# Pinning every engine to a planner's order, with four local moves, in a two-layer encoder

## The chip, the core and the metric

One core of one Trainium2 chip runs the whole program. The metric is the device time of one execution in microseconds (us); the time of a kernel is the median over its runs. The engines are named as in the profile: PE (TensorE, matrix products and transposes), ACT (ScalarE), DVE (VectorE), POOL (GpSimd) and SP (SyncE, which here only issues transfers).

## The reference

Two layers on 512 tokens of width 1024, batch 1, in float32. Each layer has four steps, each closed by a layer norm:

```
for i in range(2):
    y = swiglu(x, ffn_w_gate[i,0], ffn_w_up[i,0], ffn_w_down[i,0])    # hidden width 2816
    x = layer_norm(ALPHA*x + 0.5*y, ...)
    y = mixer_ab(x, ...) if i == 0 else mixer_c(x, ...)
    x = layer_norm(ALPHA*x + y, ...)
    y = memory_attn(x, mem, mem_w_q[i], mem_w_kv[i], mem_w_o[i])      # 4 heads into 256 memory tokens
    x = layer_norm(ALPHA*x + y, ...)
    y = swiglu(x, ffn_w_gate[i,1], ffn_w_up[i,1], ffn_w_down[i,1])
    x = layer_norm(ALPHA*x + 0.5*y, ...)
```

mixer_ab has 8 dense heads (RMS-normed, rotated q and k, 2 key heads) and 8 heads in a window of 128 tokens with a sink logit; mixer_c is a 2-D neighbourhood attention with 16 heads and a relative bias.

## The kernel before

Every float32 operand of a product is split into a rounded high part and a low part (ACT casts the high part, DVE subtracts it for the low part), and a product is three matmuls: high·high, high·low, low·high (`mm3`). x lies in four token tiles `x0` to `x3` of 128x1024; its transposes, which feed the projections, lie split in `xh` and `xl`, written by `to_features` (8 PE transposes a tile, two casts, two subtractions).

The stages run one after another: `ffn` four times, `mixer_ab` and `mixer_c` once, `memory` twice. A stage ends in `down`, which adds the last output projection to each x tile and closes it with `layer_norm` and `to_features`, tile by tile.

Weights come by SP through two large `raw` buffers (1 MB), are split into `slab` buffers, and are then used from there. There are 27 slabs of 128x1024, handed out first in, first out, in the order in which the program asks; a request waits until a slab is free. PSUM has 3 banks of kind `a`, 3 of `t` and 2 of `d`. The names in the profile are those of these buffers: `t` is also the name of the small SBUF tiles (`t2`).

Nothing is issued when the Python code runs. `Graph.record` writes down each operation with its dependencies and a cost in ns (`cost`); `emit` then plays the program as a list schedule: each engine takes, among what is ready, the operation that was written first, and `LATENCY` is added between engines. The operations are handed to the framework in the order that results. The framework's own scheduler then places them again, so that an engine's final order is not everywhere that of the planner. All recorded operations have the line of the recorder (L140), so that rows are told apart by their tiles.

At the start, `ffn_by_tokens` loads x0, then the first gate and up weights in halves, then x1 to x3, and works token tile by token tile. In `mixer_ab`, tile by tile, the keys and queries go through `rms` (square on ACT, sum on DVE, `rsqrt`, product on DVE) and `rope` (three products on DVE, a sum on POOL); `keys` and `queries` then transpose them. `padded` gives two zeroed tiles, by POOL memsets. `rsqrt` is two POOL steps, mean and eps (`tensor_scalar`) and `pow` against the constant `nhalf`. In the loop over 16 heads, `aside[n]` lists what is done behind head n: `last_columns` (the second half of the queries, four tiles, in `d` banks; its last step copies values out of the bank on ACT), shares of the output projection, and so on. In `mixer_c` the key and query parts are moved across partitions by SP's transfers (`slab<-t`), on the same queue as the weights. `memory` begins with the load of the memory, 16 transposes and 4 split pairs, behind the mixer's `down` in the order of the program.

Of the kernel before, what the change touches and what calls it, by code (L numbers as in the profile page):

```python
# [12 lines left out]
F32 = mybir.dt.float32  # L13
# [4 lines left out]
ALU = mybir.AluOpType  # L18
# [45 lines left out]
class Graph:  # L64
# [1 line left out]

    LATENCY = 90.0
    PATIENT = ("vector", "scalar")  # L70
    ENGINES = ("tensor", "vector", "scalar", "gpsimd", "sync")

    def __init__(self, nc):
        self.nc = nc
        self.ops, self.spaces, self.tiles = [], {}, {}
        for e in self.ENGINES:
            setattr(self, e, Recorder(self, e))
        self.banks, self.after = None, None
# [30 lines left out]
    @staticmethod  # L109
    def cost(engine, method, out, ins, kw):  # L110
        n = 1
        for d in (out if method != "tensor_reduce" else ins[0]).ap[1:]:
            n *= d[1]
        wide = any(z.space == bass.MemoryType.PSUM for z in ins + [out]) if engine != "sync" else False
        if method == "dma_start":
            return max(n * out.ap[0][1] * 4 / 205.0, 600.0) if engine == "sync" else 700.0
        if engine == "tensor":
            return max(n / 2.4 + 14, 111)
        small = sum(1 for z in ins if z.ap[-1][1] == 1 and n > 1)
        if engine == "vector":  # L120
            if method in ("tensor_copy", "tensor_scalar") and not wide:
                n = n / 2
            return n / 0.96 + 72 + 60 * ("accum_out" in kw)
        if engine == "scalar":
            return n / 1.2 + (90 if wide else 130) + 45 * small + 130 * ("accum_out" in kw)
        return n * {"tensor_scalar": 2.85, "memset": 1.0}.get(method, 2.17) + 110

    def record(self, engine, method, args, kw):
        kw = dict(kw)
# [35 lines left out]
    def emit(self):  # L165
        for info in self.tiles.values():
            info["left"] = len(info["users"])
            for op in info["users"]:
                op.frees.append(info)
        now = {e: 0.0 for e in self.ENGINES}  # L170
        heaps = {e: [] for e in self.ENGINES}
        ready = {e: [] for e in self.ENGINES}
        for op in self.ops:
            op.wait = len(op.deps) + len(op.frees)
            op.ready = 0.0
            for d in op.deps:
                d.users.append(op)

        def release(op, t):
            op.ready = max(op.ready, t)  # L180
            op.wait -= 1
            if op.wait == 0:
                heapq.heappush(heaps[op.engine], (op.ready, op.rank, op.index, op))

        def grant(space):

            while space.next < len(space.queue) and space.free:
                info = space.queue[space.next]
                space.next += 1
                if info["users"]:  # L190
                    t = heapq.heappop(space.free)
                    for op in info["users"]:
                        release(op, t)

        def arrive(e):
            while heaps[e] and heaps[e][0][0] <= now[e]:
                _, rank, i, op = heapq.heappop(heaps[e])
                heapq.heappush(ready[e], (rank, i, op))

        for op in self.ops:  # L200
            if op.wait == 0:
                heapq.heappush(heaps[op.engine], (0.0, op.rank, op.index, op))
        for space in self.spaces.values():
            grant(space)
        done = 0
        self.stats = []
        while done < len(self.ops):
            best = None
            for e in self.ENGINES:
                arrive(e)  # L210
                if ready[e] and e in self.PATIENT:
                    rank, _, op = ready[e][0]
                    for at, r, _, _ in heapq.nsmallest(4, heaps[e]):
                        if at < now[e] + op.ns * 0.6 and r < rank - 40:
                            now[e] = at
                            arrive(e)
                            break
                if ready[e]:
                    t = now[e]
                elif heaps[e]:  # L220
                    t = heaps[e][0][0]
                else:
                    continue
                if best is None or t < best[0]:
                    best = (t, e)
            assert best, "no instruction can start"
            t, e = best
            if not ready[e]:
                now[e] = t
                continue  # L230
            _, _, op = heapq.heappop(ready[e])
            op.call()
            self.stats.append((e, t, op))
            now[e] = t + op.ns
            end = now[e] + {"sync": 2000.0, "tensor": 160.0}.get(e, 4000.0 if op.dma else 70.0)
            done += 1
            for u in op.users:
                release(u, now[e] if e == u.engine == "tensor" else end + self.LATENCY)
            touched = set()
            for info in op.frees:  # L240
                info["left"] -= 1
                info["at"] = max(info.get("at", 0.0), end)
                if info["left"] == 0:
                    heapq.heappush(info["space"].free, info["at"] + self.LATENCY)
                    touched.add(info["space"])
            for space in touched:
                grant(space)


class Kernel:  # L250
    def __init__(self, ctx, tc, a, out):
        self.tc, self.a, self.out = tc, a, out
        self.nc = Graph(tc.nc)
        pool = lambda name, bufs, **kw: ctx.enter_context(tc.tile_pool(name=name, bufs=bufs, **kw))
        self.cst = pool("cst", 1)
        self.big = pool("big", 1)
        self.t2p = pool("t2p", 1)
        self.slp = pool("slp", 1)
        self.raw = pool("raw", 2)
        self.sm = pool("sm", 8)  # L260
        self.psp = self.nc.banks = pool("psp", 8, space=bass.MemoryType.PSUM)
        self.dram = pool("dram", 1, space=bass.MemoryType.DRAM)
        self.n = 0
# [105 lines left out]
    def rsqrt(self, sums, n, tag, mean, eps):  # L369

        nc = self.nc
        y = self.small(n, tag + "y")
        nc.gpsimd.tensor_scalar(y, sums, mean, eps, ALU.mult, ALU.add)
        nc.gpsimd.tensor_tensor(out=y, in0=y, in1=self.nhalf[:, :n], op=ALU.pow)
        return y

# [23 lines left out]
    def layer_norm(self, t, st, gb):  # L400

        nc = self.nc
        g, b = gb
        x = self.x[t]
        nmu = self.small(1, "nmu")
        nc.vector.tensor_scalar(nmu, st[:, 0:1], st[:, 1:2], -1.0 / D, ALU.add, ALU.mult)
        var = self.small(1, "var")
        nc.scalar.activation(self.junk, x, AF.Square, bias=nmu, scale=1.0, accum_out=var)
        r = self.rsqrt(var, 1, "ln", 1.0 / D, LN_EPS / ALPHA**2)
        nc.vector.scalar_tensor_tensor(out=x, in0=x, scalar=nmu, in1=g, op0=ALU.add, op1=ALU.mult)  # L410
        nc.vector.scalar_tensor_tensor(out=x, in0=x, scalar=r, in1=b, op0=ALU.mult, op1=ALU.add)

    def down_bank(self, acts, wts, t, h, coef, tag="d"):

# [47 lines left out]
    def ffn_by_tokens(self, wg, wu, first, dst):  # L462

        if first:
            self.load_x(0)
            self.to_features(0)
            self.nc.after = self.nc.ops[-1], {"scalar", "vector"}
        gate, up = self.w_cols_k(wg, 0), self.w_cols_k(wu, 0)
# [207 lines left out]
    def mixer_ab(self, ln_i, last):  # L676
# [189 lines left out]
        vb, kB, wa, acts, q = self.padded(), [], {}, [], [None]  # L866
        aside.setdefault(5, []).append(lambda: (values_turned(), kB.extend(keys(kb, True))))
        aside[6] = [values_b]
        for n in range(8):
            h, t = divmod(n, 4)  # L870
            if t == 0:
# [42 lines left out]
    def mixer_c(self, ln_i, last):  # L914
# [153 lines left out]
        for pair in range(8):  # L1068
# [16 lines left out]
            if pair < 6:  # L1085
                for t in range(2):
                    values(pair // 2 + 1, 2 * (pair % 2) + t)
            elif pair == 6:
                share(2)
        gb = self.load_ln(ln_i)  # L1090
        self.down(acts[4:], self.w_rows(w_out, 512) + self.w_rows(w_out, 768), 1.0 / ALPHA, {"gb": gb, "last": last})


    def memory(self, i, ln_i, last):
        nc, a = self.nc, self.a
        w_q, w_kv, w_o = a["mem_w_q"][i], a["mem_w_kv"][i], a["mem_w_o"][i]
        mt = []
        raw = self.tile(self.raw, [P, 2, D], F32, "raw")
        nc.sync.dma_start(out=raw, in_=a["mem"].rearrange("(m p) d -> p m d", p=P))
        for kk in range(4):  # L1100
            ps = self.transposed(
                [(j * 256 + m * P, P, raw[:, m, (2 * kk + j) * P : (2 * kk + j + 1) * P]) for j in range(2) for m in range(2)]
            )
            mt.append(self.split_t2(ps))
        memT = lambda k, lo, hi: [z[:, (k % 2) * 256 + lo : (k % 2) * 256 + hi] for z in mt[k // 2]]
        def project(head):

# [182 lines left out]
```

## Time and profile before

| | us |
|---|---|
| median of 3 runs | 2258.34 |
| lowest, highest run | 2257.48, 2258.69 |
| profiled execution, first to last instruction (its span) | 2256.3 |
| around the span, against the median of the runs | 2.0 |
| PE busy | 2206.4 |
| DVE busy | 1395.8 |
| ACT busy | 863.3 |
| POOL busy | 286.1 |
| mean granted PE clock | 0.996 |

A row of the time order reads: start, duration (merged over a run of like instructions), engine, line, operation, out<-in, shapes, xcount, and in brackets the idle time ahead of it with what ended it. The duration of merged matmuls includes the pipeline's tail, so that it is a little over count times pitch.

### The profile page before, as it was taken

What the parts mean: (1) busy time and instruction counts of PE and PEld (TensorE: products, weight loads), DVE (VectorE), ACT (ScalarE), POOL (GpSimd) and SP (SyncE); (2) the same over time, 40 slices, a digit from 0 to 9 for tenths busy, and PEclk for the clock granted to TensorE, in tenths of its full rate; (3) what the DMA queues carried; (4) which work ended last, traced back from release to release, by engine and by line L of the source; (5) the groups of instructions that cost most, each with busy time, mean ns of one, the idle gap of its engine ahead of it and who ended that gap; (6) DMA issues with size and microseconds to landing.
All of it is one profiled execution on the core that took longest, in us unless ns stands there. A gap on an engine that the chain in (4) does not pass through costs nothing.

```text
span 2256.3 us, 28354 instructions
## 1 busy us (share of the span) xinstructions
PE 2206.4 (98%) x11312; PEld 1873.9 (83%) x11312; DVE 1395.8 (62%) x2084; ACT 863.3 (38%) x1386; POOL 286.1 (13%) x391
## 2 busy tenths in 40 slices
PE   8999999899999999999999999999999999999998
PEld 7888888778798888888888888898888988888886
DVE  5666646678745756666565667366666457666653
ACT  4323333367443433333333233245544334333331
POOL 0000203434000100002100002023411001000011
PEclk9999999999999999999999999999999999999999
DMA  6333241002433331225212334235453433322241
GB/s 206 129 119 112 68 153 57 19 19 58 132 126 116 112 109 60 76 94 186 87 42 96 117 112 149 75 107 146 120 163 96 131 112 113 112 77 72 86 140 38
DMA packets 176436, 233.69 MB, mean 104 GB/s; under 512 B 7728, under 2 KB 138416, under 8 KB 176304
## 3 DMA queue, kind: packets, MB, share of 16 engines
q1 hardware_dynamic: 173232, 221.39, 31.1%
q0 software_dynamic: 3072, 10.49, 1.4%
q8 instruction: 89, 1.46, 0.3%
q14 instruction: 43, 0.35, 0.0%
HBM read 217.17 MB, written 4.19 MB: 98 GB/s over the span
## 4 chain that ended last, share of the span: by engine, by line
PE 92%; DVE 3%; ACT 2%; DMA 1%; POOL 1%; issue 1%; SPq 0%; POOLq 0%; DVEq 0%; ACTq 0%
PE a L140 55%; PE d L140 25%; PE t L140 12%; DVE slab L140 1%; DVE x L140 1%; POOL lny L140 1%; DMA slab<-t 1%; ACT junk L140 0%; DMA x<-x 0%; ACT t L140 0%; DVE t L140 0%; ACT slab L140 0%; SPq L140 0%; DMA raw<-mem_w_kv 0%; ACT xh L140 0%
## 5 line engine op out<-in xcount | busy, mean ns | idle before, releaser
L140 PE MATMUL a<-xh,slab 128*128 128x512 f32 (+1 forms) x2960 | 890.6, 382 | 0.0
L140 PEld LDWEIGHTS a<-xh,slab 128*128 128x128 f32 x2960 | 549.1, 188 | 107.0
L140 PE MATMUL d<-slab,slab 128*128 128x512 f32 (+2 forms) x2432 | 571.7, 384 | 4.3 <-DVE slab L140 1.9
L140 PE MATMUL a<-xl,slab 128*128 128x512 f32 (+1 forms) x1480 | 565.1, 382 | 0.0
L140 PEld LDWEIGHTS d<-slab,slab 128*128 128x128 f32 x2432 | 442.2, 189 | 92.9 <-DVE slab L140 4.2
L140 ACT CAST slab<-raw 128x1024 fp32r<-128x1024 f32 x316 | 320.9, 1050 | 313.4 <-DMA raw<-ffn_w_gate 144.8
L140 DVE TENSOR_TENSOR slab<-raw,slab 128x1024 fp32r<-128x1024 f32 x316 | 391.0, 1252 | 73.7 <-ACT slab L140 56.1
L140 PEld LDWEIGHTS a<-xl,slab 128*128 128x128 f32 x1480 | 278.3, 188 | 53.2
L140 DVE TENSOR_TENSOR slab<-slab,slab 128x1024 fp32r<-128x1024 f32 (+2 forms) x208 | 241.2, 1183 | 19.6 <-ACT slab L140 17.8
L140 ACT CAST slab<-slab 128x1024 fp32r<-128x1024 f32 (+1 forms) x144 | 140.1, 1000 | 237.8 <-DVE slab L140 237.5
L140 PE MATMUL a<-slab,slab 128*128 128x256 f32 (+3 forms) x1336 | 204.5, 302 | 11.7 <-DMA slab<-t 3.8
L140 ACT CAST slab<-t 128x512 fp32r<-128x512 f32 (+2 forms) x233 | 127.5, 570 | 209.6 <-DVE t L140 144.7
L140 DVE TENSOR_TENSOR slab<-a,t 128x512 f32<-128x512 f32 x56 | 38.7, 692 | 268.2 <-PE a L140 268.2
L140 PEld LDWEIGHTS a<-slab,slab 128*128 128x128 f32 x1336 | 178.8, 192 | 27.0 <-DVE slab L140 6.5
L140 DVE SCALAR_TENSOR_TENSOR x<-d,x 128x512 f32<-128x512 f32 x216 | 147.4, 685 | 48.0 <-PE d L140 47.1
L140 DVE TENSOR_TENSOR slab<-t,slab 128x512 fp32r<-128x512 f32 (+2 forms) x233 | 145.3, 648 | 24.6 <-ACT slab L140 23.8
L140 PE MATMUL t<-slab,slab 128*128 128x512 f32 (+1 forms) x648 | 151.8, 379 | 0.0
L140 POOL TENSOR_TENSOR x<-x,slab 128x512 f32<-128x512 f32 x24 | 46.0, 1947 | 834.6 <-DVE x L140 834.6
L140 ACT ACTIVATE t<-a 128x512 f32<-128x512 f32 (+3 forms) x105 | 58.1, 553 | 219.9 <-PE a L140 218.9
L140 PEld LDWEIGHTS t<-slab,slab 128*128 128x128 f32 x648 | 115.7, 188 | 24.8 <-DVE slab L140 2.1
L140 POOL TENSOR_TENSOR t<-t,l 128x256 f32<-128x256 f32 (+2 forms) x104 | 85.1, 834 | 335.8 <-DVE l L140 321.1
L140 PE MATMUL a<-slab,xh 128*128 128x256 f32 (+1 forms) x432 | 98.6, 321 | 4.0 <-ACT xh L140 3.9
(104 smaller groups left out, 1803.8 us busy)
## 6 DMA issues: line engine op xcount, KB each, us to landing
raw<-ffn_w_gate SPq DMA_DIRECT2D x40, 1024.0 KB
raw<-ffn_w_up SPq DMA_DIRECT2D x40, 1024.0 KB
slab<-ffn_w_down SPq DMA_DIRECT2D x64, 512.0 KB
raw<-ffn_w_down SPq DMA_DIRECT2D x12, 1024.0 KB
slab<-t SPq DMA_DIRECT2D x96, 128.0 KB
raw<-mem_w_kv SPq DMA_DIRECT2D x8, 1024.0 KB
raw<-mem_w_kv SPq DMA_DIRECT2D x16, 512.0 KB
raw<-mem_w_q SPq DMA_DIRECT2D x8, 1024.0 KB
```

The source lines that it names most:

```text
L140: op.call = lambda: fn(*args, **kw)
```

## The change

Six edits, all in how the work is ordered or placed; every product is the same.

1. The planner's costs and latencies are other numbers (two of the lines are shown).
2. `emit` hands each operation over with `keep_in_program_order`, so that each engine's final order is the planner's.
3. The first step of `rsqrt` is a DVE instruction, 40 in all.
4. `layer_norm` writes (x + nmu)·g into a new slab `y` instead of into x, ahead of `rsqrt`.
5. Twenty transposes of the identity into one bank stand on PE ahead of x0's.
6. `memory_turned` (load, transposes and splits of the memory) is a function of its own, called behind head 14 of `mixer_ab` and behind pair 6 of `mixer_c`.

```diff
-    LATENCY = 90.0
+    LATENCY = {"tensor": 55.0, "vector": 36.0, "scalar": 36.0, "gpsimd": 85.0, "sync": 60.0}
...
-            return max(n * out.ap[0][1] * 4 / 205.0, 600.0) if engine == "sync" else 700.0
+            return max(n * out.ap[0][1] * 4 / 300.0, 600.0) if engine == "sync" else 600.0
...
-            op.call()
+            self.tc.keep_in_program_order(op.call())
...
-        nc.gpsimd.tensor_scalar(y, sums, mean, eps, ALU.mult, ALU.add)
+        nc.vector.tensor_scalar(y, sums, mean, eps, ALU.mult, ALU.add)
         nc.gpsimd.tensor_tensor(out=y, in0=y, in1=self.nhalf[:, :n], op=ALU.pow)
...
         nc.scalar.activation(self.junk, x, AF.Square, bias=nmu, scale=1.0, accum_out=var)
+        y = self.slab(F32)
+        nc.vector.scalar_tensor_tensor(out=y, in0=x, scalar=nmu, in1=g, op0=ALU.add, op1=ALU.mult)
         r = self.rsqrt(var, 1, "ln", 1.0 / D, LN_EPS / ALPHA**2)
-        nc.vector.scalar_tensor_tensor(out=x, in0=x, scalar=nmu, in1=g, op0=ALU.add, op1=ALU.mult)
-        nc.vector.scalar_tensor_tensor(out=x, in0=x, scalar=r, in1=b, op0=ALU.mult, op1=ALU.add)
+        nc.vector.scalar_tensor_tensor(out=x, in0=y, scalar=r, in1=b, op0=ALU.mult, op1=ALU.add)
...
             self.load_x(0)
+            warm = self.ps("t")
+            for n in range(20):
+                self.nc.tensor.transpose(warm[:, :P], self.ident, self.ident)
             self.to_features(0)
...
         aside[6] = [values_b]
+        aside[14] = [self.memory_turned]
...
             elif pair == 6:
                 share(2)
+                self.memory_turned()
...
+    def memory_turned(self):
         raw = self.tile(self.raw, [P, 2, D], F32, "raw")
-        nc.sync.dma_start(out=raw, in_=a["mem"].rearrange("(m p) d -> p m d", p=P))
+        self.nc.sync.dma_start(out=raw, in_=self.a["mem"].rearrange("(m p) d -> p m d", p=P))
+        self.mt = []
         for kk in range(4):
             ps = self.transposed(
                 [(j * 256 + m * P, P, raw[:, m, (2 * kk + j) * P : (2 * kk + j + 1) * P]) for j in range(2) for m in range(2)]
             )
-            mt.append(self.split_t2(ps))
+            self.mt.append(self.split_t2(ps))
```

What stands in a row on an engine, at the places that the prediction speaks of. First ACT at the start of the program, before; raw_95 and raw_100 are the first gate and up weights, xh_83 the high part of x, t_93 and t_94 x0's transposes:

```order
2 L140 CAST slab_96<-raw_95 128x1024
3 L140 CAST slab_98<-raw_95 128x1024
4 L140 CAST slab_101<-raw_100 128x1024
5 L140 CAST xh_83<-t_93 128x4x128
6 L140 CAST xh_83<-t_94 128x4x128
7 L140 CAST slab_103<-raw_100 128x1024
```

and after:

```order
2 L140 CAST xh_83<-t_94 128x4x128
3 L140 CAST xh_83<-t_95 128x4x128
4 L140 CAST slab_97<-raw_96 128x1024
5 L140 CAST slab_99<-raw_96 128x1024
6 L140 CAST slab_102<-raw_101 128x1024
7 L140 CAST slab_104<-raw_101 128x1024
```

x0's two casts have moved ahead of all four weight casts.

POOL in mixer_ab, at the keys' last two token tiles, before; rms2y is the root of the two key heads, slab_544 the dense keys, slab_540 a tile of the window queries, slab_617 and slab_618 the zeroed value tiles:

```order
47 L140 TENSOR_TENSOR rms2y_581<-rms2y_581,nhalf_89 128x2
48 L140 TENSOR_TENSOR slab_544<-t_502_583,t_501_582 128x256
49 L140 TENSOR_TENSOR slab_540<-t_504_585,t_503_584 128x4x64
50 L140 MEMSET slab_617 128x1024
51 L140 MEMSET slab_618 128x1024
52 L140 TENSOR_SCALAR rms2y_589<-rh_588 128x2
53 L140 TENSOR_TENSOR rms2y_589<-rms2y_589,nhalf_89 128x2
54 L140 TENSOR_TENSOR slab_544<-t_510_591,t_509_590 128x256
```

and after (slab_549, slab_545, slab_622 and slab_623 are the same tiles):

```order
37 L140 TENSOR_TENSOR rms2y_586<-rms2y_586,nhalf_89 128x2
38 L140 TENSOR_TENSOR slab_549<-t_507_588,t_506_587 128x256
39 L140 TENSOR_TENSOR slab_545<-t_509_590,t_508_589 128x4x64
40 L140 TENSOR_TENSOR rms2y_594<-rms2y_594,nhalf_89 128x2
41 L140 MEMSET slab_622 128x1024
42 L140 TENSOR_TENSOR slab_549<-t_515_596,t_514_595 128x256
43 L140 MEMSET slab_623 128x1024
44 L140 TENSOR_TENSOR slab_545<-t_517_598,t_516_597 128x4x64
```

The tensor_scalar has left POOL, pow stands ahead of both memsets, and the memsets stand one on each side of the keys' sum.

PE at the end of mixer_c, where the last down projection (d), the transposes of x2 and x3 and the memory's first products meet, before; raw_2727 is the memory, t_2728 to t_2734 its transposes, a_2746 and a_2748 the first key and value projections of the memory:

```order
7834 L140 MATMUL d_2721<-slab_2693,slab_2682 128x512
7835 L140 MATMUL t_2717<-ident_78,x_6_87 128x128 x4
7836 L140 MATMUL t_2718<-ident_78,x_6_87 128x128 x4
7837 L140 MATMUL t_2728<-ident_78,raw_2727 128x128 x4
7838 L140 MATMUL a_2746<-slab_2729,slab_2737 128x256
7839 L140 MATMUL a_2748<-slab_2742,slab_2729 128x256
```

and after, where a_2771 is the first of these projections:

```order
7848 L140 MATMUL d_2754<-slab_2724,slab_2712 128x512
7849 L140 MATMUL t_2750<-ident_78,x_6_87 128x128 x4
7850 L140 MATMUL t_2751<-ident_78,x_6_87 128x128 x4
7851 L140 MATMUL d_2754<-slab_2723,slab_2712 128x512
7852 L140 MATMUL a_2771<-slab_2683,slab_2762 128x256 x2
7853 L140 MATMUL a_2771<-slab_2683,slab_2763 128x256
```

The memory's transposes have left this place; between x2's and x3's transposes now stand all 48 matmuls of the first projection and 19 of the second.

More of the change, by code (lines that the diff above doesn't have):

```diff
@@ L64, with __init__ @@
 class Graph:
-    LATENCY = 90.0
+    LATENCY = {"tensor": 55.0, "vector": 36.0, "scalar": 36.0, "gpsimd": 85.0, "sync": 60.0}
     PATIENT = ("vector", "scalar")
     ENGINES = ("tensor", "vector", "scalar", "gpsimd", "sync")
-    def __init__(self, nc):
-        self.nc = nc
+    def __init__(self, tc):
+        self.tc, self.nc = tc, tc.nc
         self.ops, self.spaces, self.tiles = [], {}, {}
@@ L115, in cost @@
         if method == "dma_start":
-            return max(n * out.ap[0][1] * 4 / 205.0, 600.0) if engine == "sync" else 700.0
+            return max(n * out.ap[0][1] * 4 / 300.0, 600.0) if engine == "sync" else 600.0
         if engine == "tensor":
-            return max(n / 2.4 + 14, 111)
+            return max((n + 32) / 2.4, 110)
         small = sum(1 for z in ins if z.ap[-1][1] == 1 and n > 1)
@@ L122, in cost @@
                 n = n / 2
-            return n / 0.96 + 72 + 60 * ("accum_out" in kw)
+            return n / 0.96 + 152 + 60 * (small > 0) + 83 * ("accum_out" in kw)
         if engine == "scalar":
-            return n / 1.2 + (90 if wide else 130) + 45 * small + 130 * ("accum_out" in kw)
-        return n * {"tensor_scalar": 2.85, "memset": 1.0}.get(method, 2.17) + 110
+            return n / 1.2 + (165 if wide else 195) + 95 * small + 190 * ("accum_out" in kw)
+        return n * {"tensor_scalar": 2.85, "memset": 0.9}.get(method, 2.2) + {"memset": 60}.get(method, 180)
     def record(self, engine, method, args, kw):
@@ L231, in emit @@
             _, _, op = heapq.heappop(ready[e])
-            op.call()
+            self.tc.keep_in_program_order(op.call())
             self.stats.append((e, t, op))
             now[e] = t + op.ns
-            end = now[e] + {"sync": 2000.0, "tensor": 160.0}.get(e, 4000.0 if op.dma else 70.0)
+            late = {"sync": 2600.0, "tensor": 165.0}.get(e, 5000.0 if op.dma else 0.0)
+            end = now[e] + late
             done += 1
             for u in op.users:
-                release(u, now[e] if e == u.engine == "tensor" else end + self.LATENCY)
+                release(u, now[e] if e == u.engine and not op.dma else end + self.LATENCY[u.engine])
             touched = set()
@@ L243, in emit @@
                 if info["left"] == 0:
-                    heapq.heappush(info["space"].free, info["at"] + self.LATENCY)
+                    heapq.heappush(info["space"].free, info["at"] + 60.0)
                     touched.add(info["space"])
@@ L252, in __init__ @@
         self.tc, self.a, self.out = tc, a, out
-        self.nc = Graph(tc.nc)
+        self.nc = Graph(tc)
         pool = lambda name, bufs, **kw: ctx.enter_context(tc.tile_pool(name=name, bufs=bufs, **kw))
@@ L1089, in mixer_c @@
                 share(2)
+                self.memory_turned()
         gb = self.load_ln(ln_i)
         self.down(acts[4:], self.w_rows(w_out, 512) + self.w_rows(w_out, 768), 1.0 / ALPHA, {"gb": gb, "last": last})
[L1094 to L1097, printed above, removed]
+    def memory_turned(self):
         raw = self.tile(self.raw, [P, 2, D], F32, "raw")
-        nc.sync.dma_start(out=raw, in_=a["mem"].rearrange("(m p) d -> p m d", p=P))
+        self.nc.sync.dma_start(out=raw, in_=self.a["mem"].rearrange("(m p) d -> p m d", p=P))
+        self.mt = []
         for kk in range(4):
@@ L1103, in memory @@
             )
-            mt.append(self.split_t2(ps))
+            self.mt.append(self.split_t2(ps))
+    def memory(self, i, ln_i, last):
+        nc, a = self.nc, self.a
+        w_q, w_kv, w_o = a["mem_w_q"][i], a["mem_w_kv"][i], a["mem_w_o"][i]
+        mt = self.mt
         memT = lambda k, lo, hi: [z[:, (k % 2) * 256 + lo : (k % 2) * 256 + hi] for z in mt[k // 2]]
```

## The prediction

> **What bounds the kernel now.** I read the page's busy times first, then the busy time by stretch, then TensorE's (PE's) waits, and last the order of time at each of them.
>
> ```profile
> PE 2206.4 (98%) x11312; PEld 1873.9 (83%) x11312; DVE 1395.8 (62%) x2084; ACT 863.3 (38%) x1386; POOL 286.1 (13%) x391
> ```
>
> PE is the bound, busy for 98%. The change takes no matmul away and adds 20 transposes, so it can win only what PE loses: the time before its first useful work, its waits, and stretches of slow clock. By stretch (start:end, length, busy time and count of each engine, granted clock, DMA share, GB/s):
>
> ```profile
> 0.00:25.00 25.00, 13.84 (x85) 12.87 (x85) 8.57 (x10) 10.91 (x14) 0.72 (x7) 1.00 0.96 263
> 25.00:400.00 375.00, 374.95 (x1739) 312.14 (x1738) 231.13 (x292) 127.14 (x164) 36.16 (x38) 1.00 0.33 109
> 400.00:625.00 225.00, 211.26 (x1179) 176.61 (x1178) 171.68 (x396) 126.21 (x280) 80.42 (x125) 0.98 0.22 62
> 1475.00:1760.00 285.00, 273.39 (x1752) 246.25 (x1752) 187.03 (x380) 137.06 (x296) 74.81 (x131) 0.99 0.46 131
> 2240.00:2257.00 17.00, 5.50 (x25) 4.22 (x23) 7.70 (x13) 2.48 (x4) 3.67 (x4) 0.81 0.34 93
> ```
>
> The feed-forward stretch 25 to 400 leaves 0.05 us idle in 375: nothing to win, much to lose. The start leaves 25.00 − 13.84 = 11.2 us, mixer_ab with its boundary 13.7, mixer_c with its boundary 11.6, the tail 11.5. All gains must come from these 48 us, and from the clock, which the two mixers have at 0.98 and 0.99.
>
> **The clock.** Behind a wait of about 2 us PE runs at half clock for a while:
>
> ```profile
> 421.00:424.50 3.50, 3.50 (x11) 0.51 0.00 0
> 438.10:441.60 3.50, 3.11 (x10) 0.51 0.00 0
> 1574.80:1578.20 3.40, 3.40 (x17) 0.50 0.63 149
> 1725.00:1728.30 3.30, 3.30 (x18) 0.50 0.56 191
> ```
>
> Each such stretch does half its work: 3.4 × 0.5 = 1.7 us lost besides the wait itself.
>
> **The start.** The rows of before (the last two from the chain of waits):
>
> ```profile
> 1.01 0.29 POOL masks.py:199 TENSOR_SCALAR_AFFINE_SELECT ident<-ident 128x128 f32<-128x128 f32 x1
> 6.12 1.94 PE L140 MATMUL t<-ident,x 128*128 128x128 f32 x8 [6.12 <-DMA x<-x]
> 7.39 1.05 ACT L140 CAST slab<-raw 128x1024 fp32r<-128x1024 f32 x1 [5.39 <-DMA raw<-ffn_w_gate]
> 10.41 1.04 ACT L140 CAST slab<-raw 128x1024 fp32r<-128x1024 f32 x1 [0.46 <-DMA raw<-ffn_w_up]
> 11.36 1.07 ACT L140 CAST xh<-t 128x512 fp32r<-128x512 f32 x2
> 12.00 0.79 PE L140 MATMUL a<-slab,xh 128*128 128x256 f32 x2 [3.93 <-ACT xh L140]
> 13.83 1.22 DVE L140 TENSOR_TENSOR slab<-raw,slab 128x1024 fp32r<-128x1024 f32 x1
> 14.43 0.90 PE L140 MATMUL t<-ident,x 128*128 128x128 f32 x3 [1.08 <-DMA x<-x]
> 21.79 0.93 PE L140 MATMUL t<-ident,x 128*128 128x128 f32 x7
> 15.34 3.98 PE a L140 x22
> 23.69 2.67 PE a L140 x22
> ```
>
> x0 is turned by 8.06, but ACT casts three pieces of weights first, so its hi part xh starts at 11.36 and PE waits to 12.00. The same matmuls (last two rows) then run at 3.98 against 2.67 us, and 8 transposes take 1.94 against 0.93 for 7: half speed until about 18. The first 48 matmuls and 3 transposes of x1 end at 21.8. After, xh comes first. I work it out: the transposes end at 7.05 (0.93), and two casts of 1.07 together behind them by about 8.1; the weight casts follow as their pieces land, the first at 7.39 and the third at 10.41, 1.5 apart, so the fourth at about 11.9; DVE's lo part follows a cast with 1.22, so the last is there at 11.9 + 1.05 + 1.22 = 14.2. Twelve matmuls, a quarter of the 48, need this piece: 12 × 0.12 (2.67 / 22) = 1.4, end 15.6, and with three transposes 16.0. That is 5.8 us ahead of 21.8. Less about 0.8, since the second tile's hi parts now start when PE has nothing else: **gain 5.0**. Bounds: 3 (a wait on x as at 14.43, where x1 landed, 1.08, and 1.3 for the clock, below) to 6. The feed-forward stretch behind it is dense, so PE carries this gain to its end.
>
> The 20 warm transposes cost nothing: ident is written at 1.3, and 20 at half speed (1.94 / 8 = 0.24) take 4.9, as much as the 4.8 until x0 lands at 6.12; at worst they end a few tenths late. Do they lift the clock? Here transposes of the same kind filled a half-clock stretch:
>
> ```profile
> 1725.58 1.91 PE L140 MATMUL t<-ident,x 128*128 128x128 f32 x8
> 1727.28 1.58 PE L140 MATMUL t<-ident,raw 128*128 128x128 f32 x8
> ```
>
> From 1725.58 on PE does nothing but 16 transposes, and the clock comes back within the second eight (1.58 against 1.91). So transposes count as work, and I let the warm-up stand. The Trainium skill, "TensorE: Matmul & The Clock Gate", Part 4, says the opposite, that full clock does not engage for transposes since they don't count as busy in the same way; by that rule the start would gain about 1.3 us less, and this trace speaks against it.
>
> **Keys and values in mixer_ab.**
>
> ```profile
> 413.64 1.21 DVE L140 TENSOR_TENSOR slab<-raw,slab 128x1024 fp32r<-128x1024 f32 x1
> 415.40 1.84 POOL L140 MEMSET slab<- 128x1024 f32 x2
> 417.60 0.71 POOL L140 TENSOR_TENSOR rms2y<-rms2y,nhalf 128x2 f32<-128x2 f32 x1
> 420.09 1.09 PE L140 MATMUL t<-ident,slab 128*128 128x128 f32 x8 [2.53 <-POOL slab L140]
> 438.13 0.30 ACT L140 COPY t<-d 128x128 f32<-128x128 f32 x1
> 438.49 1.22 PE L140 MATMUL d<-slab,xh 128*128 128x512 f32 x2 [1.98 <-ACT t L140]
> 2242.62 2.88 PE L140 MATMUL d<-slab,slab 128*128 128x512 f32 x12
> ```
>
> At 420.09 the keys' transposes wait 2.53 for POOL's rotary sum; ahead of it stood a weight's lo split on DVE (1.21) and two memsets on POOL (1.84), together 3.05 > 2.53. After, the split comes later, and the memsets fall into POOL's gaps behind pow and the sum. Gain 2.53 + 1.7 of clock = **4.2** (bounds 0 and 4.2; what is late next is the memset before the next sum, 0.92, beside three DVE steps). At 438.49 the queries' first matmul needs the bank that ACT's copy at 438.13 frees, behind its softmax steps. After, it stands behind 17 more matmuls of 512 columns (0.24 each by the last row) and 8 transposes (1.09), 5 us later: 1.98 + 1.7 = **3.7** (bounds 0, 3.7). The remaining waits of the mixers, one-third to one us each, I leave as they are, a loss among them to the new waits below.
>
> **Memory turned early.** Before, loads, transposes and splits of the memory fall into the last two layer norms of each mixer:
>
> ```profile
> 600.10 3.13 PE L140 MATMUL a<-slab,slab 128*128 128x256 f32 x21 [1.22 <-DVE slab L140]
> 1722.00 0.62 PE L140 MATMUL a<-slab,slab 128*128 128x256 f32 x3 [1.90 <-ACT slab L140]
> 1724.15 1.63 PE L140 MATMUL a<-slab,slab 128*128 128x256 f32 x9 [1.53 <-DVE slab L140]
> ```
>
> With the four pairs ready, the first two kv projections (48 + 48 matmuls × 0.12 = 11.5 us) need no x and fill the wait for x2 and x3. At 1722: 1.90 + 1.53 + 1.7 of clock = 5.1, less 0.4 for a longer wait on x: **4.7** (0 to 5.1). At 575 to 625 no clock was lost; 1.22 and its small neighbours: **2.5** (0 to 4). Moved into head 14 and behind pair 6 are 16 transposes, 4 casts and 4 lo splits; DVE is 171.68 of 225 busy there, so 4 × 0.65 us of splits lie beside matmuls, or cost up to 2.6 (in the new waits below). The load passes SP ahead of two output weights; they are needed last.
>
> **SP's order in mixer_c.**
>
> ```profile
> 1561.91 3.01 SPq L140 DMA_DIRECT2D raw<-c_w_in  x2
> 1565.01 10.15 SPq L140 DMA_DIRECT2D slab<-t  x12
> 1573.49 0.33 PE L140 MATMUL a<-slab,slab 128*128 128x192 f32 x1 [1.89 <-DMA slab<-t]
> 1574.61 1.24 PE L140 MATMUL a<-slab,slab 128*128 128x192 f32 x5 [0.79 <-DMA slab<-t]
> ```
>
> Two weight loads hold SP for 3.01 before twelve key and query copies for which PE waits 1.89 + 0.79. After, the second load stands behind eight of the copies, which start about 2.6 earlier: 1.89 + 0.79 + 1.7 of clock = **4.4** (0 to 4.4).
>
> **Norm and root.** The mean-and-eps step on POOL is held by DVE's wide operation:
>
> ```profile
> 2248.05 1.28 DVE L140 SCALAR_TENSOR_TENSOR x<-x,nmu,slab 128x1024 f32<-128x1024 f32 x1 [1.37 <-ACT junk L140]
> 2248.10 1.28 POOL L140 TENSOR_SCALAR lny<-var 128x1 f32<-128x1 f32 x1 [3.60 <-ACT junk L140]
> 2246.47 0.21 DVE L140 TENSOR_SCALAR nmu<-st 128x1 f32<-128x1 f32 x1
> ```
>
> After, the wide operation runs beside ACT's square into a slab of its own, and the step costs 0.21 on DVE: 1.28 − 0.21 = **1.1** at the tail, where nothing hides it; in the other 31 norms mostly hidden. 40 steps × 0.21 = 8 us of DVE spread over a kernel in which DVE idles 860.
>
> **Costs and sum.** The pinned order cannot adapt, the norms take 32 more slabs of the same 27, and moved work meets other work. No row prices that. Nearest: of the 25.3 us that the mixers' stretches idle, 2.5 + 2.0 + 1.2 + 3.4 + 2.7 were named above, so some 13.5 are the small waits of such an order; I add a quarter, 3.4 (bounds: 13.5 lost, or as much as the quarter won, since the planner now reckons with the chip's lengths). Planner lengths alone cost nothing. Sum: 5.0 + 4.2 + 3.7 + 4.7 + 2.5 + 4.4 + 1.1 − 3.4 = 22.2. The profiled span is 2256.3, the median of the runs 2258.34, so 2.0 lie around it: 2256.3 − 22.2 + 2.0 = 2236.1, so **2236**.
>
> **Rivals.**
> - The clock rule above holds: the start stays at half speed to 18. Then the last 2.5 us of its matmuls take twice that, 1.3 less gain: 2237.4. Against it the rows at 1725.58; for it, that PE again idles some 2 us between 7 and 9.
> - New waits take the mixers' place: planner and chip differ by a microsecond or two at each place, so the 12.3 us of mixer_ab's and mixer_c's terms go to the next late operation. Left are 22.2 − 12.3 = 9.9, time 2248.4. For it: at 420 to 440 wait followed wait on ACT, POOL and DVE.
> - The pinning changes little: what ran late before runs late in the new order, the start alone wins 5.0, new waits of 3.4 eat most: 2256.7. Against it: the order has visibly moved at each place.
> - Slower: weights late in the feed-forward stages. SP now issues all four down loads of a group, which wait for free slabs, ahead of the next gate and up loads, which cannot pass them. There are 16 such groups (4 in each of 4 stages), and PE has 0.05 us of slack in 375. A wait of 3 us in each makes 48 − 22.2 = 25.8 slower, 2284; it decides from 22.2 / 16 = 1.4 us a group. Against it: ACT, which waits for these loads, is busy 127.14 of 375 and the DMA engines a third, so a load has time to be late.
>
> **How the numbers follow.** Forecast 0.42, clock rule 0.17, new waits 0.22, little change 0.11, slower 0.08. A change of this kernel under 0.2% (4.5 us: 2253.8 to 2262.8) is not told from none. Faster: 0.42 + 0.17 + 0.22 = 0.81; same 0.11; slower 0.08. The range: below, the small waits won instead of lost (6.8) and the upper ends of start and boundaries (1.0 + 0.4 + 1.5) make 22.2 + 9.7 = 31.9, 2226; above it takes in the new waits and most of the way to little change, 2254. The forecast's own range is 2226 to 2243.
>
> **What would show it.** First 256-column matmuls by 9 to 10.5 us and the first tile's 48 done by 17; warm transposes at half pitch and x0's 8 in about 1; no wait over 1 us at the keys' transposes, the queries' first matmul or on slab<-t; no half-clock stretch left in the mixers; kv projections between x2's and x3's transposes without a wait; last square to last norm step about 1.1 shorter. Wrong if PE waits on weights between 25 and 400, or if new waits over 2 us bring new half-clock stretches.

## The result and the profile after

The changed kernel takes 2235.96 us (median, 2234.03 to 2236.92), the kernel before 2258.52 in the same comparison: a ratio of 0.9902, 95% interval 0.989 to 0.9914, or 22.6 us less. The profiled execution spans 2232.3 us against 2256.3, 24.0 less.

From the page: the busy times after.

```profile
PE 2200.6 (99%) x11332; PEld 1870.4 (84%) x11332; DVE 1415.7 (63%) x2124; ACT 860.0 (39%) x1386; POOL 257.1 (12%) x351
```

PE has 20 instructions more and still less busy time, which fits less work at half clock. By stretch (start:end, length, busy time and count of each engine, granted clock, DMA share, GB/s):

```profile
0.00:25.00 25.00, 20.49 (x141) 19.59 (x142) 10.07 (x12) 11.95 (x15) 0.76 (x7) 0.93 0.97 268
25.00:400.00 375.00, 374.82 (x1719) 311.12 (x1718) 237.52 (x302) 126.38 (x163) 34.46 (x31) 1.00 0.32 103
400.00:625.00 225.00, 211.26 (x1227) 179.39 (x1226) 178.09 (x409) 129.78 (x290) 79.90 (x118) 1.00 0.23 66
1475.00:1760.00 285.00, 283.25 (x1831) 255.23 (x1830) 195.07 (x387) 143.85 (x303) 62.47 (x122) 1.00 0.50 144
```

In mixer_c's stretch the idle time fell from 11.6 to 1.8 us. In 400 to 625 PE is busy for exactly as long as before, 211.26, with 48 more matmuls: the clock is 1.00 instead of 0.98.

Since the stretches don't hold the same work, I cut both traces at the same amounts of matmul work, and sum what is lost at each place: the time from one matmul's start to the next, less the pitch at full clock (0.227 us for 512 columns, 0.120 for 256, 0.110 for a transpose). Waits and slow clock both count; the lead-in is the time ahead of x0's transposes, the 20 warm ones among it.

| us lost | before | after | won | forecast |
|---|---|---|---|---|
| lead-in and start (first 25 us of matmuls) | 15.1 | 10.8 | 4.3 | 5.0 |
| mixer_ab up to its last projection | 19.8 | 20.9 | −1.1 | 4.2 + 3.7 |
| end of mixer_ab, begin of memory | 7.2 | 1.7 | 5.5 | 2.5 |
| mixer_c | 12.1 | 5.4 | 6.7 | 4.4 |
| end of mixer_c, begin of memory | 7.6 | 0.5 | 7.1 | 4.7 |
| feed-forward stages and inside memory | 7.4 | 7.3 | 0.1 | in −3.4 |
| tail behind the last matmul | 10.8 | 9.5 | 1.3 | 1.1 |
| all | 80.0 | 56.1 | 23.9 | 22.2 |

The sum is right, its parts are not: the boundaries and mixer_c won more, mixer_ab nothing.

Each number comes from one profiled execution. Two kernels below (without the warm transposes, and with 16 more) have PE's matmuls in this kernel's order from x0's transposes to the end, and mixer_ab loses 23.4 and 22.2 there, against 20.9. So a difference of less than some 2.5 us in mixer_ab can't be told from none. Lead-in and start spread by 1.2 among the kernels with the same order of matmuls there.

The start, in order of time:

```profile
1.37 3.87 PE L140 MATMUL t<-ident 128*128 128x128 f32 x20 [1.37 <-POOL nhalf L140]
5.83 1.09 PE L140 MATMUL t<-ident,x 128*128 128x128 f32 x8 [0.59 <-DMA x<-x]
6.52 1.07 ACT L140 CAST xh<-t 128x512 fp32r<-128x512 f32 x2 [4.50 <-PE t L140]
8.59 0.38 PE L140 MATMUL a<-slab,xh 128*128 128x256 f32 x1 [1.67 <-ACT slab L140]
9.85 0.39 PE L140 MATMUL a<-slab,xh 128*128 128x256 f32 x1 [0.88 <-DVE slab L140]
17.07 1.47 PE L140 MATMUL t<-ident,x 128*128 128x128 f32 x12
```

and the stretch behind the second wait, with columns as above:

```profile
11.00:14.40 3.40, 3.40 (x19) 3.40 (x18) 2.49 (x3) 2.81 (x4) 0.00 (x0) 0.54 1.09 248
```

The warm-up fits ahead of x0, and x0's 8 transposes take 1.09 instead of 1.94. Then PE waits 1.67 and 0.88 for weights, and from 11.0 on it has 3.4 us of half clock after all. The first tile is done at 17.07, before at 21.8 with three of x1's transposes among it.

Mixer_ab, at the keys, and in the dense heads' end where new waits stand:

```profile
414.60 1.09 PE L140 MATMUL t<-ident,slab 128*128 128x128 f32 x8 [0.97 <-POOL slab L140]
418.99 0.44 PE L140 MATMUL t<-ident,slab 128*128 128x128 f32 x2 [1.00 <-POOL slab L140]
431.99 0.51 PE L140 MATMUL d<-slab,slab 128*128 128x512 f32 x1 [1.42 <-DVE slab L140]
491.15 1.68 DVE L140 TENSOR_TENSOR slab<-raw,slab 128x1024 fp32r<-128x1024 f32 x1
491.56 0.66 PE L140 MATMUL t<-ident,t 128*128 128x128 f32 x4 [1.47 <-ACT t L140]
493.48 0.66 PE L140 MATMUL t<-ident,t 128*128 128x128 f32 x4 [1.26 <-DVE slab L140]
```

The wait of 2.53 at the keys is now 0.97, a second one of 1.00 follows it at 418.99, the wait of 1.98 for the copied bank is gone and with both the half clock. But at 431.99, 491.56 and 493.48 PE waits 1.3 to 1.5 each; at 493.48 a weight's lo split (1.68) stands ahead of the split that PE needs, in DVE's fixed order.

The second memory boundary, and SP in mixer_c:

```profile
1703.50 1.03 PE L140 MATMUL t<-ident,x 128*128 128x128 f32 x8
1704.29 0.48 PE L140 MATMUL d<-slab,slab 128*128 128x512 f32 x1
1704.60 8.19 PE L140 MATMUL a<-slab,slab 128*128 128x256 f32 x67
1712.63 1.04 PE L140 MATMUL t<-ident,x 128*128 128x128 f32 x8
1554.75 5.28 SPq L140 DMA_DIRECT2D slab<-t  x8
1560.07 0.59 SPq L140 DMA_DIRECT2D raw<-c_w_in  x1
```

67 matmuls run between x2's and x3's transposes, with no wait named on any row, and eight copies are issued ahead of the weight load that stood before them.

### The profile page after: what moved, and what is told of

It is laid out like the page before. It is cut to its first block, busy times and chain, and to the rows that moved or that the text cites. A ratio compares the mean times of both kernels' runs of the same rounds, so it can differ in the third digit from the quotient of the medians.

```text
span 2232.3 us, 28333 instructions
## 1 busy us (share of the span) xinstructions
PE 2200.6 (99%) x11332; PEld 1870.4 (84%) x11332; DVE 1415.7 (63%) x2124; ACT 860.0 (39%) x1386; POOL 257.1 (12%) x351
## 3 DMA queue, kind: packets, MB, share of 16 engines
q8 instruction: 89, 1.46, 0.3%
## 4 chain that ended last, share of the span: by engine, by line
PE 92%; DVE 5%; ACT 1%; DMA 1%; POOL 0%; issue 0%; SPq 0%; POOLq 0%; ACTq 0%
PE a L140 54%; PE d L140 26%; PE t L140 12%; DVE slab L140 2%; DVE t L140 2%; ACT slab L140 1%; DMA slab<-t 0%; DMA raw<-ab_w_out 0%; POOL rms8y L140 0%; DMA x<-x 0%; ACT t L140 0%; DVE rms2y L140 0%; DVE rh L140 0%; POOL rms2y L140 0%; DVE x L140 0%
## 5 line engine op out<-in xcount | busy, mean ns | idle before, releaser
L140 DVE TENSOR_TENSOR t<-a,t 128x512 f32<-128x512 f32 (+1 forms) x25 | 17.3, 692 | 134.4 <-PE a L140 130.8
```

The source lines that it names most:

```text
L140: op.call = lambda: fn(*args, **kw)
```

## The experiments

The theory at the outset (T): the gain is a sum of places, as in the table; the pin and the lengths give the start and mixer_c, the early turning gives the boundaries, the norm gives the tail. The rival (R): pinning as such gives nearly all. A median's ratio is known to about 0.13%, 2.9 us.

### Pin alone

```diff
 kernel before, and
-            op.call()
+            self.tc.keep_in_program_order(op.call())
```

> The kernel before with the pinned order alone (old lengths, old norm, memory turned late, no warm transposes). Theory T (the gain is a sum of places: start 4.5 us by x's casts going first, two memory boundaries 13.8 by the early turning, mixer_c 7.7 by the new lengths together with the pin, tail 1.3 by the norm, mixer_ab minus 2): 2253 to 2256, only the start's 3 to 4 us gained, mixers within 3 us of before. Rival R (pinning itself brings the gain, wherever the order stands): 2240 to 2245.

Measured: 2246.91, ratio 0.9949 (0.9936 to 0.9961), 11.6 us won; between the two expectations. By places it wins 7.7 in mixer_c (12.1 to 4.4), 1.6 at the first boundary and 1.4 at the start, and nothing at the second boundary (7.5). So mixer_c's gain is the pin's alone, without the new lengths: that part of T fell. Mixer_ab loses 20.7, against 19.8 before.

### Lengths alone, and with the pin

```diff
 kernel before, and
-    LATENCY = 90.0
+    LATENCY = {"tensor": 55.0, "vector": 36.0, "scalar": 36.0, "gpsimd": 85.0, "sync": 60.0}
 (and the new cost function; for the second also the pin)
```

> The kernel before with the planner's new lengths and latencies alone, the framework's scheduler sorting again behind it. T: between 2250 and 2260, since what the planner decides is partly undone. R: 2258, no change without the pin.

> The kernel before with pin and new lengths, without the early turning, the norm's edits and the warm transposes. T: start and mixer_c remain, 4 + 7.7, less 2 in mixer_ab: 2247 to 2251, with PE's waits at both memory boundaries (6 to 7 us each) still there. R: 2238 to 2241, the boundaries' waits gone too, since the pinned order lets work move ahead there.

Measured: 2262.15, ratio 1.0018 (1.0009 to 1.0027), and 2262.81, ratio 1.0021 (1.0012 to 1.003), both outside both expectations. The new lengths make the pinned kernel 15.9 us slower than the pin alone, which neither theory had. By places, pin and lengths against pin: the feed-forward stages lose 10.9 instead of 1.2, the boundaries 17.8 instead of 13.1, and mixer_ab 22.2 instead of 20.7; the start wins 1.7.

### All but the pin

```diff
 changed kernel, and
-            self.tc.keep_in_program_order(op.call())
+            op.call()
```

> The changed kernel without the pin. T: the boundaries (13.8) and the tail (1.3) stay won, the start and a part of mixer_c are lost: 2243 to 2248. R: 2253 to 2258.

Measured: 2245.02, ratio 0.994 (0.9927 to 0.9952): T. Without the pin the start loses 10.0 beside the lead-in (with the pin 5.0): ACT again casts all four pieces of weights, from 7.13 on, ahead of x0, whose hi part starts at 12.76 instead of 6.52. Mixer_c loses 11.7 (with the pin 5.4), the boundaries stay won (1.7 and 0.5); mixer_ab is better, 16.7 instead of 20.9. In mixer_ab the framework's order beats the planner's by 4.2 us here. The runs above show that this hangs on the lengths: with the old norm and the memory late, the pin moves mixer_ab from 17.9 to 22.2 beside the new lengths, but only from 19.8 to 20.7, inside the spread, beside the old ones. What in the new lengths does it is not shown.

### No warm transposes, and more of them

```diff
 changed kernel, and for the second
             self.to_features(0)
+            fill = self.ps("t")
+            for n in range(16):
+                self.nc.tensor.transpose(fill[:, :P], self.x[0][:, :P], self.ident)
```

> The changed kernel without the 20 warm transposes. If transposes lift the clock (theory T): x0's 8 transposes take 1.9 us instead of 1.1 and the first matmuls run at half speed from 8.6 to some time between 10 and 13; since they wait for weights until 14 anyway and the clock already falls at 11 with the warm-up, at most 1 us lost: 2235.5 to 2237. Rival (the warm-up costs more than it brings, the slow stretch is moved): 2234 to 2235.5.

> The changed kernel with 16 more transposes of x0 (their result is not used) between x0's own and the first matmul, so that PE has no gap from 6.9 to 8.6 us. Theory T (the half-clock stretch from 11.0 to 14.4 us of the changed kernel comes from that gap; transposes count as work): no half clock at the start, the first tile's 48 matmuls done at 15.6 to 16 instead of 17.07, 2234.5 to 2235.5. Rival (the gap of 1 us behind the first matmul is enough, or the weights are the bound in any case): 2235.5 to 2237, the half clock still there.

Measured: 2236.13, ratio 0.9901 (0.9887 to 0.9914), and 2236.04, ratio 0.9899 (0.9886 to 0.9913): neither can be told from the changed kernel, and medians known to 2.9 us can't settle a matter of 1 us; what follows goes by the traces. Without the warm-up x0's transposes take 1.94 again and the first tile is done at 18.25 instead of 17.07:

```profile
6.27 1.94 PE L140 MATMUL t<-ident,x 128*128 128x128 f32 x8 [6.27 <-DMA x<-x]
```

With 16 more, the stretch of the start, and then its order of time:

```profile
0.00:25.00 25.00, 22.47 (x168) 21.53 (x168) 9.32 (x11) 12.04 (x16) 0.76 (x7) 1.00 0.96 269
```

```profile
5.92 2.84 PE L140 MATMUL t<-ident,x 128*128 128x128 f32 x24 [0.28 <-DMA x<-x]
15.70 1.51 PE L140 MATMUL t<-ident,x 128*128 128x128 f32 x12
23.03 2.00 ACT L140 CAST slab<-raw 128x1024 fp32r<-128x1024 f32 x2 [2.01 <-DMA raw<-ffn_w_gate]
25.56 0.50 PE L140 MATMUL a<-slab,xh 128*128 128x256 f32 x2 [0.45 <-ACT xh L140]
```

The half clock is gone, and the first tile is done at 15.70, as T said. The granted clock of 1.00 alone would not show it, since it also reads 1.00 for the start of the kernel before, where 8 transposes take 1.94; the pitch does: two matmuls of 256 columns take 0.40 throughout, where the changed kernel has 0.63 between 11.3 and 14.3. But of the 1.4 us, 1.2 are given back by 26.5: at 25.56 PE waits for the next hi part of x, and in ACT's pinned order two weight casts, which waited 2.01 for their load, stand ahead of it. Lead-in and start lose 10.7 instead of 10.8: the clock was T's, the time the rival's.

### Memory late, and memory alone

```diff
 changed kernel, and (for the second the reverse, on the kernel before)
-        aside[14] = [self.memory_turned]
...
-                self.memory_turned()
...
-        mt = self.mt
+        self.memory_turned()
+        mt = self.mt
```

> The changed kernel with the memory turned where it was before, at the start of memory. T: the two boundaries lose 6 to 7 us each, 2247 to 2250, and mixer_ab gains up to 2 back, since 16 transposes and 8 splits leave its last heads. Rival R: the pinned order had dissolved these waits by itself, 2236 to 2240.

> The kernel before with the early turning of the memory alone. T (this gain doesn't need the pin): both boundaries from 7 us of stall to 2 or less, 2246 to 2250. Rival (the framework's scheduler or the old norm fills the boundary with other waits): 2252 to 2257.

Measured: 2247.7, ratio 0.9956 (0.9944 to 0.9969), and 2248.92, ratio 0.9957 (0.9943 to 0.9971): T both times. Left out it costs 11.7, alone it wins 9.6. With the memory late the boundaries lose 9.0 and 8.2; PE's waits at the second one, engine waited for, total, times, longest:

```profile
PE t L140 <- DVE x L140: 3.6, 2, 2.3
PE a L140 <- ACT slab L140: 1.9, 1, 1.9
```

mixer_ab wins only 0.5 from the transposes that leave it (20.4 against 20.9, inside the spread), so nothing shows that they eat its gain.

### The old norm, and its product in place

```diff
 changed kernel, and for the first also the root's first step on POOL
-        y = self.slab(F32)
-        nc.vector.scalar_tensor_tensor(out=y, in0=x, scalar=nmu, in1=g, op0=ALU.add, op1=ALU.mult)
         r = self.rsqrt(var, 1, "ln", 1.0 / D, LN_EPS / ALPHA**2)
-        nc.vector.scalar_tensor_tensor(out=x, in0=y, scalar=r, in1=b, op0=ALU.mult, op1=ALU.add)
+        nc.vector.scalar_tensor_tensor(out=x, in0=x, scalar=nmu, in1=g, op0=ALU.add, op1=ALU.mult)
+        nc.vector.scalar_tensor_tensor(out=x, in0=x, scalar=r, in1=b, op0=ALU.mult, op1=ALU.add)
```

> The changed kernel with the norm as before (first step of the root on POOL, in-place product behind the square). T: 1.3 us lost at the tail, and with POOL's first step back in the rotary chain of mixer_ab 0 to 2 there, and 0 to 2 at the boundaries: 2237.5 to 2241. Rival (only the tail shows the norm): 2237.0 to 2237.5.

> The changed kernel with the norm's product in place again, behind the square, while the first step of the root stays on DVE. T (at a norm, pow on POOL is held by the wide product that now follows the step, so the separate slab is what pays at the norms, and the DVE step pays only in mixer_ab's rotary chain): the norms' part of the 13.6 us that the old norm lost, about 9, is lost, 2243 to 2247, with the tail at 10.8 instead of 9.5. Rival (taking the first step from POOL is what pays): 2236 to 2239.

Measured: 2249.53, ratio 0.9958 (0.9945 to 0.997), far above what either theory had: the norm is worth 13.6 us here, not 1.3. In place with the step on DVE: 2245.37, ratio 0.9937 (0.9924 to 0.9949), as the second expectation of T had it: most of it, 9.4, is the separate slab (of the tail's 1.3, though, only 0.9). The slab with the step on POOL was not run, so the other 4.2 is a difference and no measurement of its own. The first norm of the first stage, with the old norm:

```profile
351.91 0.19 ACT L140 ACTIVATION_READ_ACCUMULATOR junk<-x,nmu 128x1 f32 x1
352.18 1.28 POOL L140 TENSOR_SCALAR lny<-var 128x1 f32<-128x1 f32 x1 [29.21 <-ACT junk L140]
354.14 1.28 DVE L140 SCALAR_TENSOR_TENSOR x<-x,lny,slab 128x1024 f32<-128x1024 f32 x1 [0.73 <-POOL lny L140]
355.48 1.09 PE L140 MATMUL t<-ident,x 128*128 128x128 f32 x8 [0.44 <-DVE x L140]
```

and in the changed kernel:

```profile
352.00 0.18 ACT L140 ACTIVATION_READ_ACCUMULATOR junk<-x,nmu 128x1 f32 x1
352.22 0.15 DVE L140 TENSOR_SCALAR lny<-var 128x1 f32<-128x1 f32 x1
353.30 1.28 DVE L140 SCALAR_TENSOR_TENSOR x<-slab,lny,slab 128x1024 f32<-128x1024 f32 x1
354.98 1.04 PE L140 MATMUL t<-ident,x 128*128 128x128 f32 x8
```

The last step starts 2.2 us behind the start of the square's accumulator read (the first row of each) with the old norm, 1.3 with the new one, and in the old one x's transposes, which PE's order has where the planner thought them ready, wait. The same norm's `pow`, first with the product in place and the step on DVE, then in the changed kernel:

```profile
353.62 1.51 POOL L140 TENSOR_TENSOR lny<-lny,nhalf 128x1 f32<-128x1 f32 x1 [29.41 <-DVE lny L140]
352.52 0.56 POOL L140 TENSOR_TENSOR lny<-lny,nhalf 128x1 f32<-128x1 f32 x1 [23.26 <-DVE lny L140]
```

In place, the wide product (from 353.42 on) starts on DVE just ahead of pow, and pow takes 1.46 to 1.57 in all 32 norms. With the slab, the product is done by then, and pow takes 0.55 to 0.59 in 21 norms and 1.40 to 1.46 in 11. So the hold only moves from POOL's first step to its second, unless the product goes. Over the whole run (old norm; engine waited for, total, times, longest):

```profile
PE t L140 <- DVE x L140: 4.3, 14, 0.5
PE t L140 <- POOL slab L140: 2.4, 1, 2.4
```

The first wait is not in the changed kernel's list at all. By places the old norm loses 7.0 more in the feed-forward stages (3.9 of it are waits on x, 2.7 of these ahead of x's transposes; what the rest is, isn't shown), 4.1 in mixer_ab (the keys' wait is 2.4 again, so long that the half clock is back), 1.7 at the boundaries and 1.3 at the tail.

### Old lengths, and old margins

```diff
 changed kernel, and for the first the old cost function and latencies; for the second
-    LATENCY = {"tensor": 55.0, "vector": 36.0, "scalar": 36.0, "gpsimd": 85.0, "sync": 60.0}
+    LATENCY = {"tensor": 90.0, "vector": 90.0, "scalar": 90.0, "gpsimd": 90.0, "sync": 90.0}
...
-            late = {"sync": 2600.0, "tensor": 165.0}.get(e, 5000.0 if op.dma else 0.0)
+            late = {"sync": 2600.0, "tensor": 165.0}.get(e, 5000.0 if op.dma else 70.0)
```

> The changed kernel, pinned, with the old lengths and latencies in the planner. T: mixer_c's 7.7 depend on the lengths, so 2240 to 2246. Rival (what counts in mixer_c is the order of the program that the pin keeps, whatever the lengths): 2235 to 2238.

> The changed kernel with its new lengths but the old margins between engines (90 ns each, 70 behind an operation of ACT, DVE or POOL). Theory T (the new lengths' narrow margins place work so close that small delays reach PE, while the lengths themselves help only at the start): stalls of the feed-forward and memory places as with the old lengths (2.3 instead of 4 us), the start as in the changed kernel (5.0), mixer_ab 19 to 21: 2232 to 2235. Rival (the margins don't matter): 2235.5 to 2236.5.

Measured: 2235.23, ratio 0.9892 (0.9877 to 0.9907), and 2235.91, ratio 0.9908 (0.9894 to 0.9921): the rivals' numbers both times. With the new norm the lengths are worth nothing that can be told: they win 2.5 at the start (7.4 to 5.0) and lose 2.3 in the feed-forward stages and 2.0 in mixer_ab, the last inside the spread. The margins don't explain that: with wide ones the feed-forward stages lose 5.5, not less than 4.0.

The lengths and the norm together make a square of the feed-forward stages' loss, all pinned: old norm and old lengths 1.2 (with the memory late), old norm and new lengths 10.9 (11.0 with the memory early), new norm and old lengths 1.7, both new 4.0. So the new lengths cost 9.7 beside the old norm, and 2.3 beside the new one. With the product in place and the step on DVE, where `pow` is held instead, these stages still lose 8.1, so the hold matters on either step. That the new lengths leave it out (POOL's first step takes 1.28 beside DVE's product and is reckoned with 0.18) would fit, but the old lengths leave it out as well (0.11), so it does not tell the two apart. No run gave the planner the true length, and none had wide margins beside the old norm: why the hold costs PE more beside the new lengths stays open.

## Why the prediction was right, point by point

- **Bound and places.** PE is still the bound, and the gains came from places that had idle time; the feed-forward stages lost 1.6 (2.4 to 4.0), far from the rival's 1.4 a group.
- **Start.** Right in kind, 4.3 against 5.0. PE waited for the first weights at 8.59 and 9.85, which I had, and fell to half clock at 11.0; an idle PE between 7 and 9 was what the text had for the rival. That costs nothing here: filled, the time goes into the next wait. (I took 0.93, the row of seven transposes, for x0's eight; they take 1.09.)
- **Clock rule.** The warm transposes lift the clock (x0's eight in 1.09 against 1.94; the twenty take 3.87, not the 4.9 of half speed), and with 24 of x0's in a row the full pitch lasts through the start. The Trainium skill, "TensorE: Matmul & The Clock Gate", Part 4, has the full clock not engage for transposes, since they don't count as busy in the same way; for these float32 transposes both traces say otherwise. The price of the rival was about right (1.2 us at 18 us), too little for a median to show.
- **Keys and queries.** The step that failed. The two waits and their half clocks went nearly as worked out (2.53 to 0.97, 1.98 to none, no half clock between 400 and 625), but the place won −1.1 and not 7.9: I let a wait that goes count as won and left the next late work at what it was. The rival of new waits was right here: its mechanism held for mixer_ab and not for mixer_c. Pin and new lengths do it together: unpinned the same program loses 16.7 there, and pinned with the old lengths 18.9.
- **Memory.** Mis-sized, 12.6 for both boundaries against 7.2. I left 0.4 for a longer wait on x and credited the first boundary with one wait; no wait is left, since two projections fill the gap and the small neighbours go with it. By its own run the edit is worth 9.6 to 11.7.
- **SP in mixer_c.** 6.7 against 4.4, mechanism as told; the pin alone brings it.
- **Norm.** The tail was right, 1.3 against 1.1. That it is mostly hidden in the other 31 norms failed: left out it costs 13.6 beside the new lengths, where x's transposes wait for x (4.3 in all), which is a part of it; the rest is open.
- **Planner lengths alone cost nothing.** Wrong alone (3.6 slower) and with the pin (15.9 slower than the pin); beside the new norm no cost can be told.
- **New waits, −3.4.** They came in mixer_ab, and 1.6 in the feed-forward stages; inside memory 1.7 was won (5.0 to 3.3), which makes the table's 0.1.

So the places and most mechanisms were right, but that 2236 came out to the digit is luck: an error of 9 us in mixer_ab met errors of 5.4 at the boundaries, 2.3 in mixer_c and the 3.4 that I had set aside.

## What to carry to other kernels

Edits to a list schedule are not a sum: the norm's edit was worth 1.1 us on the path that I could see and 13.6 beside the new lengths, so price an edit with the other edits in place, and leave each out in turn. A pinned order pays where a queue had the wrong transfer first (SP in mixer_c) and cost 4.2 us in mixer_ab, where many short operations meet, beside one set of lengths and nothing that can be told beside the other, so try a pin with more than one; pinning by stage was not tried here. A wait taken away is won only after looking at what is late next: in mixer_ab two half-clock stretches and two waits of together 4.5 us (2.53 and 1.98) gave way to two of 1.0 and to others of 1.3 to 1.5 behind them, and the place was no faster.

## What the runs showed that I had not expected

- After 3.87 us of warm transposes and 1.09 of x0's, waits of 1.67 and 0.88 brought the clock down to 0.54 for 11.0 to 14.4; with 16 transposes in the first gap alone, it stayed at 1.00 with the 0.88 wait still there. At 491.56 and 493.48 waits of 1.47 and 1.26 in two us did not bring it down, so the sum of close waits alone doesn't decide it.
- DVE's root step on one column takes 0.15 us, not the 0.21 of the similar step I took; POOL's pow still takes up to 1.46 beside a weight's lo split on DVE (128x1024), 0.55 alone and 0.55 to 0.57 beside the 128x512 sums that read a `d` bank. So not every DVE operation holds it.
